# An encoder block on one core: its front stage in another order, its small preparations on other engines

## The chip, the cores and the metric

The kernel runs on one core of one Trainium2 chip. The metric is the device time of one execution in microseconds (us); the runs shown are three executions of the kernel before, and of them the median counts.

## What is computed

One layer of a bidirectional encoder for two sequences of 512 tokens and width 1024, all in fp32. Cut to what matters here:

```python
mod = silu(c) @ w_ada + b_ada            # conditioning: 6 x 1024 values per sequence
sh1, sc1, gt1, sh2, sc2, gt2 = split(mod, 6)
h = rmsnorm(x, g_attn) * (1 + sc1) + sh1
z = h @ w_in                             # -> qa, ka, va, cq, ckv, kr, gla, glb
qa, ka = rope(rmsnorm(qa, gq_a)), rope(rmsnorm(ka, gk_a))     # mixer A: 8 and 2 heads of 64
oa = window_attention(qa, ka, va, sink_a)
qb = rmsnorm(rmsnorm(cq, g_cq) @ w_uq, gq_b)                  # mixer B: low-rank parts, 256 wide
kv = rmsnorm(ckv, g_ckv) @ w_ukv                              # and 128 wide; 32 of a head's 96
ob = dense_attention(rope(qb), rope(norm(kv, kr, gk_b)), v)   # columns are rotated
mix = sigmoid(gla) * (oa @ w_o_a) + sigmoid(glb) * (ob @ w_o_b)
x = x + gt1 * (mix @ w_out)
# then a second modulated norm, and a gated MLP with a depthwise convolution of width 3
```

## The kernel before, in words

The engines are TensorE (PE), VectorE (DVE), ScalarE (ACT) and GpSimd (POOL); SP issues all DMAs, in order. Every fp32 operand of a large product is split into a rounded high part and the rest (hi, lo), and a product is three matmuls (mm3, L78 to L81): hi by hi, hi by lo, lo by hi. A framework takes the program's instructions, plans each engine's order by priority and a cost model of its own, gives out the buffers of a pool in turn (`bufs`), and adds the waits; each engine then runs its list strictly in order. Where a line stands in keep_in_program_order, the plan may not move it.

The front stage has these parts. Tokens lie in 8 tiles of 128 (NT = 4 for a sequence), the width in KD = 8 blocks of 128.

1. *Norm* (norm, L243): a tile of x is loaded; two ACT squares with sums, a mean, a reciprocal root by ACT's Sqrt and five DVE instructions (rsqrt, L83), and a DVE scaling (L254). The first sequence's four tiles come first, the second sequence's in steps 3 to 6 of the next part.
2. *Eight steps* (L269): step k loads 1 MB of w_ada0, makes the scale and shift of block k by 32 small matmuls (64 recorded, L281) and a transpose (L289), transposes block k of the first sequence (L104), modulates and splits it (modulated, L109), and multiplies block k - 1 by the weights of part 0 of w_in (project, L263: 12 matmuls of 416 columns into four PSUM banks). Part 0 holds cq, ckv and kr. POOL splits these weights. Behind step 7's load the rotary tables are loaded and multiplied by gains on DVE (tables, L190).
3. *Second sequence* (L301): eight blocks are transposed and modulated; in between the low-rank weights w_uq and w_ukv are loaded and split (low_rank, L218).
4. *Low-rank parts* (prep_b, L340), a generator in three stages, so that three tiles are under way: squares and roots of cq and ckv, cn = part of z by root by gain (L353) and the rotation of kr on POOL; transposes of cn (L360) and their split; products with w_uq and w_ukv, copies, squares, roots, rotation on POOL, scalings, and three DMAs to a DRAM scratch. Tiles 4 to 7 first need their own product z (z_tile, L329).
5. *Mixer A* (prep_a, L405): for part 1 and then part 2 of w_in, 384 columns each, and each tile: product z in one of two PSUM banks, ACT copy to SBUF, square, sum and root for 4 or 6 heads of 64, rotation in four DVE instructions (L324 to L327), scaling by the root (L426), DMAs to DRAM. In each of these 16 iterations stands one step of the second half of the conditioning (ada, L141): 1 MB of w_ada, four matmuls (8 recorded, L151); after eight of them an addition (L155), four transposes (L158) and copies.

Behind it the attention block begins: its tiles lie in the SBUF of parts 1 to 5. PE runs the attention of both mixers with the gate products (gates, L470, matmuls L491) spread between; POOL splits the gate weights (L69, L72). Two banks are theirs, six the attention's. Parts 1 to 3 hold all eight PSUM banks, part 5 three.

Of the kernel before, what the change touches and what calls it, by code (L numbers as in the profile page):

```python
# [8 lines left out]
F32 = mybir.dt.float32  # L9
# [30 lines left out]
def encoder_block(ctx, tc, x, c_t, w_ada0, b_col, w_ada, b_ada, cols, w_z, w_g, gains, tabs, sink,  # L40
# [18 lines left out]
    SY.dma_start(colt, cols)  # L59
# [5 lines left out]
    SY.dma_start(gcol[0:NOPE, 0:1], gains[2 * AD:2 * AD + NOPE].unsqueeze(1))  # L65
    SY.dma_start(gcol[0:NOPE, 1:2], gains[2 * AD + BQK:2 * AD + BQK + NOPE].unsqueeze(1))
# [16 lines left out]
    def rsqrt(pool, a, width):  # L83
# [43 lines left out]
    with ExitStack() as st:  # L127
# [9 lines left out]

        bcol = zp.tile([128, 2 * KD], F32, name="bcol")
        SY.dma_start(bcol, b_col)

        def ada():  # L141

            for part in range(2):
# [27 lines left out]
        def table(tc_, ts_, off, dim, g0):  # L171
# [5 lines left out]
            V.tensor_mul(tc_, tc_, bcast(g, 1, [128, NT, dim]))  # L177
            V.tensor_mul(ts_[:, :, 0:h], ts_[:, :, 0:h], bcast(g[:, h:dim], 1, [128, NT, h]))
            V.tensor_mul(ts_[:, :, h:dim], ts_[:, :, h:dim], bcast(g[:, 0:h], 1, [128, NT, h]))
# [8 lines left out]
        gbc = ur.tile([128, QL + KVL], F32, name="gbc")  # L188

        def tables():  # L190
            for m in range(2):
                table(tcb[:, :, m], tsb[:, :, m], 2 * AD, ROPE, 2 * AD + m * BQK + NOPE)
            SY.dma_start(gbc, gains[2 * AD + 2 * BQK:2 * AD + 2 * BQK + QL + KVL].partition_broadcast(128))

# [22 lines left out]

        def low_rank(k):  # L218

            rw = zp.tile([128, KD, 4, 64], F32, name="w_ada", bufs=3).rearrange("p a b c -> p (a b c)")  # L220
# [15 lines left out]
        with ExitStack() as s0:  # L236
# [6 lines left out]
            def norm(t):  # L243
                xt = wk.tile([128, D], F32, name="xt", bufs=2 * NT)
                SY.dma_start(xt, x[t * 128:(t + 1) * 128, :])
                ss = wk.tile([128, 2], F32, name="ss", bufs=4)
                for q in range(2):
                    junk = wk.tile([128, S], F32, name="tmp", bufs=2)
                    A.activation(junk, xt[:, q * S:(q + 1) * S], AF.Square, accum_out=ss[:, q:q + 1])
                r = wk.tile([128, 1], F32, name="r", bufs=4)  # L250
                V.tensor_add(r, ss[:, 0:1], ss[:, 1:2])
                mean_eps(r, r, D)
                rsqrt(wk, r, 1)
# [890 lines left out]
```

## Time and profile before

| | |
|---|---|
| runs shown | 1458.96, 1456.97, 1456.27 us; median 1456.97 |
| profiled execution | 1456.77 us, span 1455.0 us from first to last instruction |
| PE | 1391.8 us busy, 96% of the span |
| DVE, ACT, POOL | 1000.3, 679.3, 596.0 us busy |
| DMA | 193.82 MB, 133 GB/s on average |
| chain that ended last | PE 77%, DVE 13% |

The rows below are of five kinds. [...] A row of a wait names who waited for whom, the total, the number of times and the longest. A row in order of time has start, length, engine, line, operation, tiles, shapes, and in brackets the idle time before it and what ended it. A row of a group has the count behind x, the busy time, the mean of one in ns, and the idle time before them. A row of a DMA has the count, the size and the median time from issue to landing. PE's matmuls overlap, so that their lengths are longer than the distance from one to the next.

### The profile page before, as it was taken

How to read it: one execution, taken by the hardware profiler on the slowest of the kernel's cores; microseconds unless marked ns; L12 is line 12 of the kernel's file. 1: busy time of each engine (PE TensorE's matmuls, PEld its weight loads, DVE VectorE, ACT ScalarE, POOL GpSimd, SP SyncE). 2: the span in 40 equal slices, each digit the busy share in tenths (PEclk: the TensorE clock that was granted, in tenths of full speed). 3: DMA queues.
4: the chain of work that ended last, by engine and by line, in shares of the span. 5: the costliest groups of instructions: out<-in, count | busy, mean ns of one | idle time of the engine just before them, and what ended most of it. 6: DMA issues, size and time to landing. Idle time of an engine off the chain costs nothing.

```text
span 1455.0 us, 20795 instructions
## 1 busy us (share of the span) xinstructions
PE 1391.8 (96%) x7184; PEld 1153.1 (79%) x7184; DVE 1000.3 (69%) x1907; ACT 679.3 (47%) x1385; POOL 596.0 (41%) x592
## 2 busy tenths in 40 slices
PE   5888998999999999999998899999999999999998
PEld 4777776888888888878887767888888888888887
DVE  5788776666678886545479888777777787447433
ACT  3475223666666665422347455555555554212210
POOL 3174023442433442381005755555555545544430
PEclk9999999999999999999999999999999999999999
DMA  8565763322222213655312322222222327646522
GB/s 342 176 216 170 236 239 135 116 88 87 88 87 73 102 64 120 236 176 200 133 39 73 120 74 87 87 82 85 87 85 82 102 73 250 205 148 223 180 87 73
DMA packets 107801, 193.82 MB, mean 133 GB/s; under 512 B 18856, under 2 KB 39592, under 8 KB 104624
## 3 DMA queue, kind: packets, MB, share of 16 engines
q1 hardware_dynamic: 107696, 192.49, 39.8%
q8 instruction: 57, 0.93, 0.3%
q14 instruction: 48, 0.39, 0.1%
HBM read 148.39 MB, written 44.06 MB: 132 GB/s over the span
## 4 chain that ended last, share of the span: by engine, by line
PE 77%; DVE 13%; POOL 3%; ACT 2%; DMA 2%; issue 2%; SPq 0%; ACTq 0%; POOLq 0%; DVEq 0%
PE px L955 13%; PE psg L491 11%; PE py L955 7%; PE psd L79 5%; PE psd L80 5%; PE psd L81 5%; PE pz L955 3%; PE ppt L512 3%; PE ppo L575 2%; PE psx L81 2%; PE psx L80 2%; PE psx L79 2%; PE psz L79 2%; PE psy L81 1%; PE psy L79 1%
## 5 line engine op out<-in xcount | busy, mean ns | idle before, releaser
L955 PE MATMUL px<-t,wt 128*128 128x512 f32 x792 | 191.2, 391 | 7.0 <-ACT tmp_cc L960 6.3
L922 POOL TENSOR_TENSOR wt<-wraw,wt 128x512 fp32r<-128x512 f32 x66 | 92.8, 1410 | 232.2 <-ACT wt L921 232.0
L955 PEld LDWEIGHTS px<-t,wt 128*128 128x128 f32 x792 | 148.0, 188 | 41.1 <-ACT tmp_cc L960 9.5
L491 PE MATMUL psg<-h_hi,wg 128*128 128x512 f32 x512 | 170.2, 397 | 0.0
L506 POOL TENSOR_SCALAR p<-p,l 128x512 f32<-128x512 f32 (+2 forms) x128 | 78.8, 617 | 200.3 <-DVE l L505 125.7
L76 DVE TENSOR_TENSOR wd<-wraw,wd 128x512 fp32r<-128x512 f32 x88 | 93.1, 1098 | 96.4 <-ACT wd L75 96.4
L79 PE MATMUL psd<-wd 128*128 128x512 f32 x352 | 136.9, 389 | 0.0
L80 PE MATMUL psd<-wd 128*128 128x512 f32 x352 | 136.9, 389 | 0.0
L81 PE MATMUL psd<-wd 128*128 128x512 f32 x352 | 136.9, 389 | 0.0
L75 ACT CAST wd<-wraw 128x512 fp32r<-128x512 f32 x88 | 51.3, 620 | 156.1 <-issue 86.9
L491 PEld LDWEIGHTS psg<-h_hi,wg 128*128 128x128 f32 x512 | 95.9, 189 | 18.4 <-POOL wg L69 0.8
L491 PE MATMUL psg<-h_lo,wg 128*128 128x512 f32 x256 | 101.8, 397 | 0.0
L504 ACT ACTIVATE p<-pps,nm 128x512 f32<-128x512 f32 (+2 forms) x128 | 78.2, 611 | 39.3 <-DVE nm L501 31.7
L922 DVE TENSOR_TENSOR wt<-tmp_sf,wt 128x512 fp32r<-128x512 f32 x88 | 82.2, 944 | 12.2 <-ACT wt L921 12.0
L967 DVE SCALAR_TENSOR_TENSOR tmp_u<-tmp_cc,cw,tmp_u 128x511 f32<-128x511 f32 x66 | 64.3, 974 | 37.3 <-ACT tmp_u L966 37.2
L69 POOL TENSOR_SCALAR wd<-wraw 128x512 fp32r<-128x512 f32 x44 | 34.2, 777 | 112.0 <-PE psd L81 63.9
L81 PEld LDWEIGHTS psd<-wd 128*128 128x128 f32 x352 | 66.1, 188 | 13.8
L79 PEld LDWEIGHTS psd<-wd 128*128 128x128 f32 x352 | 66.1, 188 | 13.7
L80 PEld LDWEIGHTS psd<-wd 128*128 128x128 f32 x352 | 66.1, 188 | 13.6
L501 DVE TENSOR_REDUCE nm<-pps 128x1 f32<-128x512 f32 (+2 forms) x128 | 74.7, 584 | 3.1 <-PE pps L81 1.5
L966 ACT ACTIVATE tmp_u<-tmp_cc,cw 128x512 f32<-128x512 f32 x66 | 53.6, 813 | 45.7 <-DMA g_d<-tmp_u 25.6
L72 POOL TENSOR_TENSOR wd<-wraw,wd 128x512 fp32r<-128x512 f32 x44 | 72.7, 1653 | 3.7
(257 smaller groups left out, 3517.8 us busy)
## 6 DMA issues: line engine op xcount, KB each, us to landing
w_ada<-in_w_ada_dram SPq DMA_DIRECT2D x24, 1024.0 KB, 7.1
wraw<-in_w_up_dram SPq DMA_DIRECT2D x96, 256.0 KB, 2.7
wraw<-in_w_down_dram SPq DMA_DIRECT2D x88, 256.0 KB, 3.6
g_d<-tmp_u SPq DMA_DIRECT2D x44, 256.0 KB, 2.4
wraw<-g_d SPq DMA_DIRECT2D x44, 256.0 KB, 2.7
wg_raw<-in_w_g_dram SPq DMA_DIRECT2D x16, 512.0 KB, 3.7
gate_d<-go SPq DMA_DIRECT2D x32, 256.0 KB, 2.0
ldb<-qb_d SPq DMA_DIRECT2D x8, 1024.0 KB, 4.9
```

Source lines behind the costliest of these rows:

```text
L72: G.tensor_sub(lo, raw, hi.bitcast(F32))
L76: V.tensor_sub(lo, raw, hi.bitcast(F32))
L79: PE.matmul(ps, lhsT=lh, rhs=rh, start=first, stop=False)
L80: PE.matmul(ps, lhsT=lh, rhs=rl, start=False, stop=False)
L81: PE.matmul(ps, lhsT=ll, rhs=rh, start=False, stop=last)
L491: PE.matmul(ps, lhsT=w[:, wl, m, k, :], rhs=hl[b][:, k, :], start=k == 0 and n == 0, stop=k == KD - 1 and n == 2)
L501: V.tensor_reduce(nm, ps[:, :n], op=ALU.max, axis=AX.X, negate=True)
L504: A.activation(p[:, :n], ps[:, :n], AF.Exp, bias=nm, accum_out=l)
L506: G.tensor_scalar(out=p[:, :plen], in0=p[:, :plen], scalar1=l, scalar2=1.0, op0=ALU.mult, op1=ALU.mult)
L922: lo_eng.tensor_sub(w[:, 1], raw, w[:, 0].bitcast(F32))
L955: PE.matmul(ps[:, sl], lhsT=w[:, wl, i], rhs=h[:, hl, sl], start=not add and i == 0 and n == 0, stop=i == 3 and n == 2, skip_group_check=add)
L967: V.scalar_tensor_tensor(out=u[:, 1:S], in0=src[:, 0:S - 1], scalar=cw[:, cc, 0:1], in1=u[:, 1:S], op0=ALU.mult, op1=ALU.add)
```

## The change

The front stage is rebuilt. The x loads go ahead of the small ones; 60 transposes of the identity stand on PE's list ahead of the steps. Norms are made for two tiles at a time (first sequence) and four (second), with the scalings partly on ACT and the root by two instructions less. The squares' outputs go to tiles that are written later. The tables are multiplied on POOL, later. The gains of cq and ckv are folded into the low-rank weights' split, and cn becomes two ACT copies. The conditioning's second half runs between the low-rank parts, two steps per tile, its loads three ahead. The weights of parts 1 and 2 are loaded in two large pieces into the buffers of w_ada, and split later. Mixer A reads PSUM directly: four banks more, ACT scales each head by its root, DVE and POOL share the rotation, and the closing product is gone.

```diff
     def rsqrt(pool, a, width):
...
-        V.tensor_mul(u, a, y)
+        V.scalar_tensor_tensor(out=u, in0=a, scalar=-0.5, in1=y, op0=ALU.mult, op1=ALU.mult)
         V.tensor_mul(u, u, y)
-        V.tensor_scalar(out=u, in0=u, scalar1=-0.5, scalar2=1.5, op0=ALU.mult, op1=ALU.add)
-        V.tensor_mul(a, y, u)
+        V.scalar_tensor_tensor(out=a, in0=u, scalar=1.5, in1=y, op0=ALU.add, op1=ALU.mult)
...
         def ada():
+            ws = []
+            def load():
+                n = len(ws)
+                if n < 2 * KD:
+                    w = zp.tile([128, KD, 4, 64], F32, name="w_ada", bufs=3).rearrange("p a b c -> p (a b c)")
+                    SY.dma_start(w, w_ada[n // KD, n % KD])
+                    ws.append(w)
+            load()
+            load()
+            yield
             for part in range(2):
...
                 for k in range(KD):
-                    w = zp.tile([128, KD, 4, 64], F32, name="w_ada", bufs=3).rearrange("p a b c -> p (a b c)")
-                    SY.dma_start(w, w_ada[part, k])
+                    load()
+                    w = ws[part * KD + k]
...
-            V.tensor_mul(tc_, tc_, bcast(g, 1, [128, NT, dim]))
+            G.tensor_mul(tc_, tc_, bcast(g, 1, [128, NT, dim]))
...
+        def weights_late(part):
+            c0, cw = ZC[part]
+            raws = []
+            for k in range(0, KD, 4):
+                raw = zp.tile([128, KD, 4, 64], F32, name="w_ada", bufs=3).rearrange("p a b c -> p (a b c)")[:, :4 * cw]
+                raw = raw.rearrange("p (k n) -> p k n", k=4)
+                SY.dma_start(raw, w_z[:, k:k + 4, c0:c0 + cw])
+                raws.append(raw)
+            def split():
+                tiles = []
+                for k in range(KD):
+                    w, raw = zp.tile([128, 2, ZB], F32R, name="wz", bufs=10), raws[k // 4][:, k % 4]
+                    A.copy(w[:, 0, :cw], raw)
+                    (V if k % 2 else G).tensor_sub(w[:, 1, :cw], raw, w[:, 0, :cw].bitcast(F32))
+                    tiles.append(w)
+                return tiles
+            return split
...
-                tc.keep_in_program_order(A.copy(hi, raw))
-                tc.keep_in_program_order(V.tensor_sub(lo, raw, hi.bitcast(F32)))
+                tc.keep_in_program_order(A.activation(hi, raw, AF.Copy, scale=g))
+                tc.keep_in_program_order(V.scalar_tensor_tensor(out=lo, in0=raw, scalar=g, in1=hi.bitcast(F32),
+                                                                op0=ALU.mult, op1=ALU.subtract))
...
+            for t in range(NT):
+                load_x(t)
+            SY.dma_start(colt, cols)
+            SY.dma_start(bcol, b_col)
+            one = wk.tile([128, 1], F32, name="one")
+            V.memset(one, 1.0)
+            tc.keep_in_program_order(A.activation(one, one, AF.Sqrt))
+            for t in range(0, NT, 2):
+                ss = wk.tile([128, 2], F32, name="ss", bufs=2)
+                for j in range(2):
+                    xt = xn[t + j].rearrange("p (a n) -> p a n", a=2)
+                    A.activation(h_lo[1][:, 2 * (t + j):2 * (t + j) + 2, :], xt, AF.Square, accum_out=ss[:, j:j + 1])
+                r = scales(ss)
+                V.tensor_scalar(out=xn[t], in0=xn[t], scalar1=r[:, 0:1], scalar2=None, op0=ALU.mult)
+                if t:
+                    A.activation(xn[t + 1], xn[t + 1], AF.Copy, scale=r[:, 1:2])
+                else:
+                    V.tensor_scalar(out=xn[t + 1], in0=xn[t + 1], scalar1=r[:, 1:2], scalar2=None, op0=ALU.mult)
+            idle = pst.tile([128, S], F32, name="pst")
+            for j in range(60):
+                PE.transpose(idle[:, (j % NT) * 128:(j % NT + 1) * 128], ident, ident)
...
-                xt = transposed(pst, xn[:NT], k, True)
+                xt = transposed(pst, xf[:NT], k, True)
+                if k:
+                    project(k - 1, 0, 2)
...
                 if k:
-                    project(k - 1)
+                    project(k - 1, 2, NT)
...
+                if 2 <= k < 6:
+                    t = NT + k - 2
+                    A.activation(h_hi[1][:, 2 * (k - 2):2 * (k - 1), :], xn[t].rearrange("p (a n) -> p a n", a=2), AF.Square,
+                                 accum_out=ss1[:, k - 2:k - 1])
+                if k == 5:
+                    r1 = scales(ss1)
+                    for t in range(NT):
+                        A.activation(xn[NT + t], xn[NT + t], AF.Copy, scale=r1[:, t:t + 1])
...
-                    V.scalar_tensor_tensor(out=cn[:, c0:c1], in0=zt[:, c0:c1], scalar=rc[:, j:j + 1], in1=gbc[:, c0:c1],
-                                           op0=ALU.mult, op1=ALU.mult)
+                    A.activation(cn[:, c0:c1], zt[:, c0:c1], AF.Copy, scale=rc[:, j:j + 1])
...
+                for h in range(n):
+                    A.activation(zs[:, h], zh[:, h], AF.Copy, scale=rs[:, h:h + 1])
...
+                V.tensor_mul(t1, zv, tc_)
+                G.tensor_mul(t2[lo], zv[hi], ts_[lo])
+                G.tensor_mul(t2[hi], zv[lo], ts_[hi])
+                V.tensor_add(ov, t1, t2)
...
             for t in range(2 * NT + 2):
+                for _ in range(2):
+                    next(mods, None)
+                if t == 2 * NT - 1:
+                    later = weights_late(1)
                 if t < 2 * NT:
                     stages.append(prep_b(t, zfirst[t] if t < NT else z_tile(t, tiles, ZC[0][1])))
...
+                if t == 2 * NT:
+                    tiles = later()
...
+            pza = s0.enter_context(tc.tile_pool(name="pza", bufs=4, space=PSUM))
+            later = weights_late(2)
             for part in range(2):
-                tiles = weights(1 + part)
                 for t in range(2 * NT):
-                    prep_a(t, z_tile(t, tiles, ZC[1 + part][1]), part)
-                    next(mods, None)
-            for _ in mods:
-                pass
+                    zt = z_product(pza, t, tiles, ZC[1 + part][1])
+                    if not part and t == 2 * NT - 1:
+                        tiles = later()
+                    prep_a(t, zt, part)
```

## Rows read from the trace of the kernel before

**Rows 1.** Busy time of each engine by stretch, then clock, DMA share, GB/s.
```profile
14.50:61.10 46.60, 38.84 (x656) 33.16 (x657) 31.12 (x103) 14.47 (x34) 14.01 (x16) 0.96 0.71 255
...
61.10:75.10 14.00, 12.85 (x74) 10.71 (x71) 12.82 (x26) 10.25 (x24) 4.22 (x9) 1.00 0.82 288
...
75.10:140.50 65.40, 56.04 (x288) 47.56 (x288) 56.49 (x163) 43.49 (x117) 41.94 (x73) 0.97 0.54 179
...
140.50:216.30 75.80, 75.43 (x448) 59.55 (x446) 56.56 (x211) 19.82 (x53) 10.23 (x12) 1.00 0.75 244
...
216.30:225.50 9.20, 3.07 (x17) 2.35 (x14) 9.10 (x12) 0.34 (x2) 9.20 (x10) 0.78 0.49 170
...
225.50:400.00 174.50, 174.49 (x924) 145.41 (x923) 112.23 (x225) 107.38 (x227) 62.32 (x82) 0.99 0.29 100
...
10.00:40.00 30.00, 21.35 (x395) 18.30 (x395) 21.12 (x71) 11.83 (x32) 10.83 (x12) 1.00 1.02 401
```

**Rows 2.** Waits of PE, 75 to 232 us: us, times, longest.
```profile
PE ppr L360 <- DVE cn L353: 8.9, 6, 3.0
...
PE psa L158 <- DVE br L155: 6.1, 1, 6.1
```

**Rows 3.** PE in order of time, first steps: start, length, line, count.
```profile
14.52 1.94 PE L281 MATMUL pa<-w_ada,c_s 128*32 128x64 f32 x64 [14.52 <-DMA w_ada<-in_w_ada_dram]
...
21.90 1.11 PE L104 MATMUL pst<-ident,xt 128*128 128x128 f32 x4
...
25.77 1.10 PE L281 MATMUL pa<-w_ada,c_s 128*32 128x64 f32 x64
...
26.80 0.66 PE L104 MATMUL pst<-ident,xt 128*128 128x128 f32 x4
...
29.76 1.10 PE L281 MATMUL pa<-w_ada,c_s 128*32 128x64 f32 x64
```

**Rows 4.** As rows 1, stretches for the clock.
```profile
14.50:23.50 9.00, 6.72 (x139) 5.25 (x140) 6.76 (x19) 0.98 (x2) 5.16 (x7) 1.00 1.01 414
...
48.00:50.00 2.00, 2.00 (x49) 1.79 (x41) 0.41 (x2) 0.00 (x0) 0.00 (x0) 0.50 0.06 13
...
224.70:228.30 3.60, 3.54 (x11) 2.96 (x12) 3.57 (x14) 0.00 (x0) 2.18 (x2) 0.51 0.14 50
```

**Rows 5.** SP and PE in order of time, at the start.
```profile
3.55 1.85 SPq L245 DMA_DIRECT2D xt<-in_x_dram  x4
...
19.41 0.48 PE L104 MATMUL pst<-ident,xt 128*128 128x128 f32 x1 [2.12 <-DVE xt L254]
```

**Rows 6.** Groups of ACT, 75 to 140.5 us: count, busy us, mean ns.
```profile
L346 ACT ACTIVATE jc<-zo 128x128 f32<-128x128 f32 x7 | 2.1, 303 | 0.1
```

**Rows 7.** Groups of DVE, 75 to 140.5 us.
```profile
L353 DVE SCALAR_TENSOR_TENSOR cn<-zo,rc,gbc 128x256 f32<-128x256 f32 x8 | 5.7, 712 | 0.0
...
L353 DVE SCALAR_TENSOR_TENSOR cn<-zo,rc,gbc 128x128 f32<-128x128 f32 x8 | 3.6, 446 | 0.0
```

**Rows 8.** PE in order of time, conditioning beside mixer A.
```profile
199.10 1.07 PE L151 MATMUL psa<-w_ada,c_s 128*32 128x512 f32 x8
...
204.50 1.06 PE L151 MATMUL psa<-w_ada,c_s 128*32 128x512 f32 x8
```

**Rows 9.** DMA issues: count, KB each, median us to landing.
```profile
w_ada<-in_w_ada_dram SPq DMA_DIRECT2D x24, 1024.0 KB, 7.1
```

**Rows 10.** As rows 1, two tiles of mixer A.
```profile
199.70:205.10 5.40, 5.40 (x40) 4.32 (x32) 3.65 (x13) 1.21 (x3) 0.00 (x0) 1.00 0.87 293
...
210.50:219.90 9.40, 8.13 (x49) 5.93 (x41) 9.18 (x13) 1.73 (x4) 9.40 (x11) 1.00 0.23 75
```

**Rows 11.** Groups of DVE, 199.7 to 205.1 us.
```profile
L426 DVE TENSOR_TENSOR oa<-oa,rs 128x384 f32<-128x384 f32 x1 | 0.6, 558 | 0.0
```

**Rows 12.** Groups of POOL, 75 to 140.5 us.
```profile
L324 POOL TENSOR_TENSOR t1b<-qf,tcb 128x256 f32<-128x256 f32 x8 | 8.3, 1037 | 5.6 <-ACT qf L380 5.6
...
L325 POOL TENSOR_TENSOR t2b<-qf,tsb 128x128 f32<-128x128 f32 x8 | 4.4, 549 | 0.0
```

More of the change, by code (lines that the diff above doesn't have):

```diff
@@ L187, in encoder_block @@
         tsa = zp.tile([128, NT, 2, AD], F32, name="tsa")
-        gbc = ur.tile([128, QL + KVL], F32, name="gbc")
+        glr = zp.tile([128, 3], F32, name="glr")
         def tables():
@@ L241, in encoder_block, with load_x @@
             xn = [None] * (2 * NT)
-            def norm(t):
+            def load_x(t):
                 xt = wk.tile([128, D], F32, name="xt", bufs=2 * NT)
                 SY.dma_start(xt, x[t * 128:(t + 1) * 128, :])
[L246 to L253, printed above, removed]
-                V.tensor_scalar(out=xt, in0=xt, scalar1=r, scalar2=None, op0=ALU.mult)
-                xn[t] = lambda k, xt=xt: xt[:, k * 128:(k + 1) * 128]
@@ L257, in encoder_block, with scales, part_of @@
-            for t in range(NT):
-                norm(t)
+                xn[t] = xt
+            def scales(ss):
+                n = ss.shape[1]
+                r = wk.tile([128, 4], F32, name="r", bufs=3)[:, :n]
+                mean_eps(r, ss, D)
+                rsqrt(wk, r, n)
+                return r
+            def part_of(t):
+                return lambda k: xn[t][:, k * 128:(k + 1) * 128]
+            xf = [part_of(t) for t in range(2 * NT)]
+            for t in range(NT):
+                load_x(t)
@@ L267, in project, with second_batch @@
                         k == 0, k == KD - 1)
+            ss1 = wk.tile([128, NT], F32, name="ss1")
+            r1 = None
+            second = iter(range(KD))
+            def second_batch():
+                k = next(second, None)
+                if k is not None:
+                    modulated(wk, transposed(pst, xf[NT:], k), 1, a1, 0, h_hi[1], h_lo[1], k)
             for k in range(KD):
@@ L299, in encoder_block @@
                 modulated(wk, xt, 0, a1, 0, h_hi[0], h_lo[0], k)
-            project(KD - 1)
-            for k in range(KD):
-                split = low_rank(k // 2) if k % 2 == 0 else split
-                modulated(wk, transposed(pst, xn[NT:], k), 1, a1, 0, h_hi[1], h_lo[1], k)
-                if k % 2:
-                    split()
+                if 2 <= k < 6:
+                    t = NT + k - 2
[5 more added lines that the diff above has]
+                        A.activation(xn[NT + t], xn[NT + t], AF.Copy, scale=r1[:, t:t + 1])
+                if k == 7:
+                    second_batch()
+            project(KD - 1, 0, NT)
+            mods = ada()
+            splits = [low_rank(n) for n in range(2)]
+            tables()
+            for k in range(0, KD, 2):
+                if k == 4:
+                    splits += [low_rank(n) for n in range(2, 4)]
+                second_batch()
+                second_batch()
+                splits[k // 2]()
+            next(mods)
+            SY.dma_start(gcol[0:NOPE, 0:1], gains[2 * AD:2 * AD + NOPE].unsqueeze(1))
+            SY.dma_start(gcol[0:NOPE, 1:2], gains[2 * AD + BQK:2 * AD + BQK + NOPE].unsqueeze(1))
+            G.tensor_scalar(out=gcol[:, 1:2], in0=gcol[:, 1:2], scalar1=BQK ** 0.5, scalar2=1.0, op0=ALU.mult, op1=ALU.mult)
             zfirst = []
```

78 lines of the change are left out of this document (41 added, 37 removed).

## The prediction

> **What bounds the kernel now.** First the busy time by stretch [rows 1]. After 225.5 us TensorE (PE) is busy without a hole: 174.49 of 174.5 us up to 400. What fills it there are the gate products, which wait for nothing that the attention does; so a front stage that ends earlier should move everything behind it forward by the same amount, and the whole question is how early PE becomes dense. Before that, PE starts at 14.5 and is idle (length less busy time) for 7.8 us up to 61.1, 1.2 up to 75.1, 9.4 up to 140.5, 0.4 up to 216.3, and 6.1 of the 9.2 us up to 225.5: 24.8 us.
>
> Second the waits [rows 2]. The 9.4 us of the third stretch are almost all one wait: the transposes of the low-rank parts wait for the scaled rows cn, and VectorE (DVE) makes those late; it is busy 56.5 of 65.4 us there. The 6.1 us are another single wait: the last conditioning transposes (L158) stand in PE's queue and wait for one addition (L155) on DVE.
>
> Third the first steps of PE in order of time [rows 3], beside the granted clock [rows 4]. The 64 small conditioning matmuls of a step take 1.94 us in the first two steps (one is shown) and 1.10 from the third on; the four transposes of a step 1.11, then 0.66. In the first 9 us the clock row says 1.00, but these durations are those of the lower level, which the other rows show as 0.50; I go by the durations. The lower level costs 2 x (0.84 + 0.45) = 2.6 us in the first two steps, and about half of three later stretches of some 3.5 us each (two are shown, the third is at 116): 5.2. With the idle time PE loses 24.8 + 7.8 = 32.6 us in the front, and 14.5 before it begins. That is all there is to win.
>
> **The change part by part.** The profiled execution took 1456.77 us with a span of 1455.0; the median of the runs shown is 1456.97, 0.2 above it. The sum is made against 1456.77.
>
> *Start.* Four small DMAs go from in front of the x loads, which are issued at 3.55 us [rows 5]; four issues take 1.85 us there, so at most 1.9 us are won. Nothing is won if the 60 added transposes still hold PE when the first weights land. At the lower level one follows the other by about 0.21 us ((1.11 - 0.48) / 3, [rows 3, 5]), so 60 take 12.7 us from about 1.7: until 14.4, today's start. At the higher one they are done at about 10. The chain in front of the first transposes also shortens: today the fourth waits 2.1 us, until 19.41, for DVE's scaling of x [rows 5]; now sums and roots go two tiles at a time, the function table is loaded ahead, and one of the four scalings goes to ScalarE (ACT). I take 1.5 between the ends 0 and 1.9.
>
> *The eight steps of conditioning and projection.* They last 46.6 us from 14.5 to 61.1. A step with nothing in its way takes 29.76 - 25.77 = 4.0 us [rows 3]; eight make 32, the last chain from the transposes to the modulated block some 2.7 (0.66 and four instructions of about half a microsecond, an estimate), the last projection 2.3, what is left of a step without the small matmuls and transposes: 37. The norms of the second sequence, which ran one tile at a time through ACT and DVE between the steps, become one square per step, one root for four tiles and four ACT scalings; the tables leave this stage. Late next are the loads: 14.3 MB (4.2 of x, 8.4 of w_ada0, 1.7 of w_z) at 401 GB/s [rows 1] are 35.7 us, so the last weights land near 39, about when PE wants them (13 + 7 x 4.0 = 41). And the four 1024-wide scalings, each under 2.4 us by the 0.30 that ACT takes for 128 columns [rows 6], queue on ACT in front of step 6. I keep 2.5 us for both: 39.5, a gain of 7; ends 0 (loads and ACT late as before) and 9.6.
>
> *Second sequence.* Its scalings are in the stage above; transposes and splits stay, and the gains are folded into w_uq and w_ukv at the same number of instructions. Twelve table products leave DVE (12.8 of 14.0 us busy) and run on GpSimd (POOL), where they can slow DVE. I take 0; ends -3 (DVE slowed by a quarter) and +1.2 (all of the idle time).
>
> *Low-rank parts.* Per tile DVE loses the two cn products, 0.71 + 0.45 us [rows 7], and three or four tiny instructions of the roots and means; some 1.7 us, 14 over eight tiles: 56.5 falls to 42. ACT gets two copies for cn; 0.30 for the 128-wide one [rows 6], at most twice that for the 256-wide, so 0.9 x 8 = 7: 43.5 rises to 51. The sixteen conditioning steps move in, two per tile. A step costs PE 1.2 us: 1.07 and the gap ahead of it [rows 8]. A tile of mixer A with its step takes 5.40, without it 4.2, so 14 of the 16 tiles fit into today's 75.8 us behind 140.5; the other two and their 8 us, which fill holes here, go out, and 14 steps come in: PE has 56 + 17 - 8 = 65 us of work and more to do while cn is made. Sixteen loads of 1 MB come along, in three buffers, 7.1 us each to landing [rows 9]: three in flight make 2.4 us each, 38 for sixteen, so they fit; but each step stands in PE's queue and, if late, holds the low-rank products and the z tiles behind it, and SP's queue holds the loads among the writes of q, k and v. Of the 11.1 us lost here (9.4 idle, 1.7 of clock) I take 5 as won; ends -6 (eight steps late by 0.8 each) and 11.1.
>
> *Mixer A.* Its 16 tiles cost PE 4.2 us each instead of 5.4, which is only the 1.2 that moved. DVE's 3.65 us of busy time per tile [rows 10] lose the closing product, 0.56 [rows 11], and two half-wide ones, together the same: 2.5. POOL gets the two half-wide products, at 192 columns between 0.55 and 1.04 each [rows 12], 1.6 together. ACT gets six copies of 64 columns, each under 0.30, and has 1.21 today, 3.0 in all. Everything lies under 4.2, so PE stays the bound and the cost is 0. New is the border: the first weights of part 1 are loaded behind the last conditioning step, into its buffers, and their splits stand behind the low-rank work on ACT and DVE; PE has one tile's low-rank products to cover it. I charge 2; ends 0 and 5. The case that the three engines do not keep up is a rival below.
>
> *Tail.* With the conditioning early, L155 and L158 are out of the way: 6.1 idle and 1.8 of clock. Late next is the end of mixer A. Its four PSUM banks come on top of the three of this stage, so seven of eight are held until ACT has copied the last tiles out, and one of the two banks of the gate products may wait for that: square, reduction, root, five tiny DVE instructions, six copies, about 4 us behind the last product by the rows named. POOL must also split the first gate weights among its new products. I take 4 of 7.9 as won; ends 0 and 7.9.
>
> Sum: 1.5 + 7 + 0 + 5 - 2 + 4 = 15.5, so 1456.8 - 15.5 = 1441.3, say **1441**. All good ends together are 32 us (1425), all bad ones -14 (1471); as six parts rarely fall to one side, the likely case has 1433 to 1448.
>
> **The rivals.**
>
> *The transposes do not warm PE.* For it: the second step still runs at the lower level. Against: the higher one comes at about 23.5, when PE had done little but small matmuls and transposes since 20. If it holds, PE starts at 14.4 (1.4 lost) and the two slow steps stay (2.6), of which the loads hide part: 1444. [...]
>
> *The low-rank stage does not shorten.* ACT in order with 51 us, or sixteen loads that hold PE's queue, take the place of DVE. For it: DVE and ACT pass each tile back and forth, and the wait for cn would only change its name. Against: no engine but PE would be over 80% busy. Price: the 5 us and 2 more at the border, 1448; with the tail's stall kept too, 1452.
>
> *Slower: DVE stretched by POOL in mixer A.* Where POOL is busy all the time, from 210.5 to 219.9, DVE needs 9.2 us for the 13 instructions that it does in 3.65 beside an idle POOL [rows 10]: 2.5 times. If its 2.5 us stretched as much, a tile would take 6.3 instead of 4.2 and, with four banks full, hold PE: 16 x 2.1 = 33 us, so 1474. It decides where a tile passes 5.2 us, as 16 x 1.0 eats the gain. Against: POOL would be busy 1.6 of 4.2 us, in which DVE does 0.6 of its 2.5; 3.5 us is what the rows give. [...]
>
> *More than forecast.* Nearly all idle time goes: 1425 to 1433. For it: PE has filler everywhere; against: new dependences in every part.
>
> **How the numbers follow.** Forecast 0.50; cold transposes 0.13; low-rank stage unchanged 0.17; more 0.08; slower, by POOL or another stall of that size, 0.12. Within 0.2% (2.9 us, about what a measurement can tell from no change) lies a fifth of the low-rank case and a little of the last: same 0.05; slower 0.10; faster 0.85. The range leaves out the slow end and the best one: 1429 to 1455.
>
> **What would show it.** First small matmuls at 12 to 13 us and 1.1 us long (1.9: the cold rival). The eighth step's projection ends near 52, not 61. The wait for cn falls under 5 us. No wait of PE for L155. Mixer A's tiles follow each other by 4.2 to 4.4 us; 5 or more is the slow rival. PE is dense from about 210. The forecast is wrong if the front ends early but PE has holes behind it, or if PE waits for w_ada in the low-rank stage for more than a few us.

## The result: 0.9% slower, where 1.1% faster was forecast

The changed kernel takes 1472.28 us (median of 4 runs, 1469.09 to 1475.48), the kernel before 1457.24 beside it (4 runs); the ratio is 1.0094, interval 1.0076 to 1.0112. The forecast was 1441 in a range of 1429 to 1455. (The ratio is the one on record; the quotient of the medians, 1.0103, differs a little.) The profiled execution took 1471.41 us, 14.6 more than that of before.

The busy time by stretch of the changed kernel, columns as in [rows 1]: the two ends and the length, then for PE, PEld (weight loads), DVE, ACT and POOL the busy time and the instructions, then PE's granted clock as a share of full speed, the busy share of the DMA engines and GB/s:

```profile
139.50:197.80 58.30, 49.65 (x239) 46.82 (x240) 38.76 (x96) 17.27 (x69) 33.40 (x42) 0.85 0.46 138
197.80:223.40 25.60, 25.60 (x147) 25.32 (x145) 11.39 (x36) 9.50 (x39) 7.63 (x10) 1.00 0.11 32
223.40:240.00 16.60, 3.29 (x9) 2.58 (x9) 6.82 (x23) 5.39 (x23) 4.51 (x6) 0.57 0.13 39
240.00:400.00 160.00, 160.00 (x845) 133.50 (x844) 99.38 (x193) 97.50 (x206) 57.68 (x77) 0.99 0.28 95
```

PE is dense from 240.0; before it was from 225.5 [rows 1]. The 14.5 us between are the whole loss, and they arise behind 139.5, in mixer A. By then all sixteen conditioning steps are done, and none of the sixteen tiles; before, 14 tiles with a step each lay behind 140.5. The sixteen tiles are 16 x 4.2 = 67.2 us of PE's work, so PE could have been dense at 206.7, 18.8 earlier than before. It gets there 33.3 us later than that: 8.7 idle in the first row (length less busy time), 13.3 idle in the third, whose 3.3 busy are gate products already, and 49.65 + 25.60 - 67.2 = 8.0 more than 4.2 a tile. Most of that goes with the granted clock, which is 0.85 on average in the first row: 0.50 from 139 to 143 and from 183 to 195, each time behind a wait of PE, and 1.00 from 195 to 223. Matmuls of 384 columns follow each other by 0.32 us at 0.50 (from 188 on) and by 0.17 or 0.18 at 1.00 (from 196 on); half of the 13.2 us that PE is busy at 0.50 makes an estimate of 6.6 of the 8.0. The waits of PE up to 262 us (us, times, longest) name the places:

```profile
PE psg L592 <- ACT zs L503: 13.3, 1, 13.3
PE psz L76 <- DVE h_hi L109: 6.1, 4, 2.5
PE psz L76 <- ACT vf L465: 5.3, 1, 5.3
PE psz L76 <- ACT wz L236: 4.2, 2, 3.7
PE psz L76 <- ACT v L527: 3.0, 2, 1.9
...
PE psa L164 <- DVE br L161: 0.9, 1, 0.9
...
PE ppr L443 <- ACT cn L437: 0.9, 2, 0.5
```

The wait for vf, the copy that empties the bank of the last low-rank tile, ends at 139.51, ahead of the first row. The 8.7 idle in that row are the waits for wz, the split weights (the longest ends at 183.39, at the border between part 1 and part 2), and for v, the last copy out of a bank of mixer A. The last two lines are what the forecast wanted: the wait for cn falls from 8.9 to 0.9, that for L155 (now L161) from 6.1 to 0.9 [rows 2]. The first line is new: the first gate product needs a PSUM bank that ACT has not yet emptied, and ACT empties the last tiles late, because the tiles come late. ACT, DVE and POOL in part 2 of mixer A, each in order of time:

```profile
208.61 1.34 ACT L503 ACTIVATE zs<-psz,rs 128x64 f32<-128x64 f32 x6 [0.92 <-DVE rs L88]
209.80 0.52 ACT L492 ACTIVATE sq<-psz 128x384 f32<-128x384 f32 x1
212.84 0.21 ACT L84 ACTIVATE rsq_y<-rs 128x6 f32<-128x6 f32 x1 [2.52 <-DVE rs L499]
213.97 1.34 ACT L503 ACTIVATE zs<-psz,rs 128x64 f32<-128x64 f32 x6 [0.92 <-DVE rs L88]
```
```profile
210.02 0.97 POOL L517 TENSOR_TENSOR t<-zs,tsa 128x192 f32<-128x192 f32 x1 [3.84 <-ACT zs L503]
210.96 0.59 POOL L518 TENSOR_TENSOR t<-zs,tsa 128x192 f32<-128x192 f32 x1
```
```profile
209.98 0.56 DVE L516 TENSOR_TENSOR t<-zs,tca 128x384 f32<-128x384 f32 x1 [1.46 <-ACT zs L503]
211.58 0.56 DVE L519 TENSOR_TENSOR oa<-t,t 128x384 f32<-128x384 f32 x1 [1.04 <-POOL t L518]
212.05 0.55 DVE L494 TENSOR_REDUCE rs<-sq 128x6 f32<-128x384 f32 x1
212.63 0.17 DVE L499 TENSOR_SCALAR rs<-rs 128x6 f32<-128x6 f32 x1
213.08 0.19 DVE L85 RECIPROCAL rsq_y<-rsq_y 128x6 f32<-128x6 f32 x1 [0.28 <-ACT rsq_y L84]
...
213.71 0.17 DVE L88 SCALAR_TENSOR_TENSOR rs<-rsq_u,rsq_y 128x6 f32<-128x6 f32 x1
```

Read it as one ring. ACT scales a tile out of PSUM (zs, 1.34); POOL makes its two products (0.97 + 0.59); DVE adds (0.56) and only then reduces the squares of the *next* tile, which ACT wrote at 209.80 and which have lain there for 1.7 us; then the root on ACT (0.21), four small instructions on DVE, and ACT may scale that next tile, at 213.97. From 208.61 that is 5.36 us, and all tiles of part 2 follow each other by 5.33 to 5.46. No engine is busy half of it: DVE 11.39 of 25.6 us, ACT 9.50, POOL 7.63 in the second row above. Every duration is undisturbed; the engines take turns. PE, with 4.2 us of work per tile, runs ahead into the four banks: its last product is done at 223.4, the last tile leaves its bank only from 235.36 on, and until then PE stands.

Part 1 has a shorter ring (four heads) and still takes 6.3 to 6.5 us a tile (zs at 164.40, 170.94, 177.26; the next, with POOL free of splits, comes 4.31 later). There POOL also splits gate weights, which the planner has put between its products. First the groups of DVE from 156 to 181 us, then one of these kinds in part 2 (count, busy us, mean ns), then POOL in order of time:

```profile
L519 DVE TENSOR_TENSOR oa<-t,t 128x256 f32<-128x256 f32 x5 | 4.0, 807 | 3.8 <-POOL t L518 3.8
L87 DVE TENSOR_TENSOR rsq_u<-rsq_u,rsq_y 128x4 f32<-128x4 f32 x3 | 3.6, 1213 | 0.1
L86 DVE SCALAR_TENSOR_TENSOR rsq_u<-rs,rsq_y 128x4 f32<-128x4 f32 x4 | 2.8, 702 | 0.1
...
L85 DVE RECIPROCAL rsq_y<-rsq_y 128x4 f32<-128x4 f32 x4 | 0.7, 178 | 1.1 <-ACT rsq_y L84 1.1
```
```profile
L87 DVE TENSOR_TENSOR rsq_u<-rsq_u,rsq_y 128x6 f32<-128x6 f32 x7 | 1.2, 166 | 0.2
```
```profile
166.74 1.36 POOL L66 TENSOR_SCALAR wg<-wg_raw 128x512 fp32r<-128x512 f32 x2
168.08 2.55 POOL L69 TENSOR_TENSOR wg<-wg_raw,wg 128x512 fp32r<-128x512 f32 x2
171.95 0.70 POOL L517 TENSOR_TENSOR t<-zs,tsa 128x128 f32<-128x128 f32 x1 [1.32 <-ACT zs L503]
```

L87 works on 4 elements per partition (6 in part 2), and takes 1.21 us beside the splits and 0.17 without them; 1.21 is about the length of one L69 on POOL (2.55 for two). The reciprocal, with one input, stays at 0.18 beside the same L69 (at 168.50 and 174.83); not every instruction with one input does (last section).

### The profile page after: what moved, and what is told of

The parts are those of the page before. It is cut to its first block, busy times and chain, and to the rows that moved or that the text cites. A ratio compares the mean times of both kernels' runs of the same rounds, so it can differ in the third digit from the quotient of the medians.

```text
span 1469.6 us, 20912 instructions
## 1 busy us (share of the span) xinstructions
PE 1403.4 (95%) x7244; PEld 1165.1 (79%) x7244; DVE 971.3 (66%) x1734; ACT 697.8 (47%) x1458; POOL 611.8 (42%) x633
## 4 chain that ended last, share of the span: by engine, by line
PE 73%; DVE 10%; issue 4%; POOL 4%; ACT 2%; DMA 2%; ACTq 0%; POOLq 0%; DVEq 0%; SPq 0%
PE px L1056 13%; PE psg L592 11%; PE py L1056 6%; PE psd L78 5%; PE psd L76 5%; PE psd L77 5%; PE pz L1056 3%; PE ppt L613 3%; PE ppo L676 2%; PE psx L76 2%; PE psx L77 2%; PE psx L78 2%; PE psy L78 2%; PE psy L76 1%; PE psy L77 1%
## 5 line engine op out<-in xcount | busy, mean ns | idle before, releaser
L592 PE MATMUL psg<-h_hi,wg 128*128 128x512 f32 x512 | 171.0, 400 | 13.3 <-ACT zs L503 13.3
L1023 DVE TENSOR_TENSOR wt<-tmp_sf,wt 128x512 fp32r<-128x512 f32 x88 | 85.2, 977 | 11.8 <-ACT wt L1022 11.4
L1068 DVE SCALAR_TENSOR_TENSOR tmp_u<-tmp_cc,cw,tmp_u 128x511 f32<-128x511 f32 x66 | 63.7, 965 | 35.4 <-ACT tmp_u L1067 35.4
L76 PE MATMUL psz<-wz,h_hi 128*128 128x384 f32 (+1 forms) x176 | 64.8, 369 | 19.0 <-DVE h_hi L109 6.1
L1070 DVE SCALAR_TENSOR_TENSOR tmp_u<-tmp_cc,cw,tmp_u 128x511 f32<-128x511 f32 x66 | 74.2, 1124 | 1.4
```

The source lines that it names most:

```text
L76: PE.matmul(ps, lhsT=lh, rhs=rh, start=first, stop=False)
L592: PE.matmul(ps, lhsT=w[:, wl, m, k, :], rhs=hl[b][:, k, :], start=k == 0 and n == 0, stop=k == KD - 1 and n == 2)
L1023: lo_eng.tensor_sub(w[:, 1], raw, w[:, 0].bitcast(F32))
L1068: V.scalar_tensor_tensor(out=u[:, 1:S], in0=src[:, 0:S - 1], scalar=cw[:, cc, 0:1], in1=u[:, 1:S], op0=ALU.mult, op1=ALU.add)
L1070: V.scalar_tensor_tensor(out=u[:, 0:S - 1], in0=src[:, 1:S], scalar=cw[:, cc, 2:3], in1=u[:, 0:S - 1], op0=ALU.mult, op1=ALU.add)
```

## Experiments

Two theories stood at the start. *Ring*: mixer A's pace is a ring through three engines' queues, closed by the order of the instructions. *Contention*: DVE is slow because POOL works beside it. A third, that the chain starts late (its first square waits 5.1 us, until 152.35, for a buffer that a write still reads), came beside them. The table gives each kernel's median and its ratio to the kernel before, with its interval; the medians of before were 1457.4 to 1458.5 in the four sets. The ratios are those on record; quotients of the medians differ from them by up to 0.002 (0.9908 for e10).

| kernel | us | ratio |
|---|---|---|
| changed kernel | 1472.3 | 1.0094 [1.0076, 1.0112] |
| e1 old mixer A in the new front | 1450.1 | 0.995 [0.993, 0.997] |
| e2 lines moved | 1471.3 | 1.0091 [1.0075, 1.0108] |
| e3 new mixer A in the old front | 1474.2 | 1.0108 [1.0087, 1.0130] |
| e4 all products on DVE | 1464.6 | 1.0048 [1.0031, 1.0066] |
| e5 no transposes | 1471.6 | 1.0085 [1.0062, 1.0109] |
| e6 order forced | 1457.4 | 0.9989 [0.9975, 1.0003] |
| e7 e6, gate splits moved | 1449.2 | 0.9946 [0.9928, 0.9963] |
| e8 gate splits moved alone | 1468.9 | 1.0070 [1.0048, 1.0093] |
| e9 e7, first tiles' banks | 1450.0 | 0.9929 [0.9901, 0.9956] |
| e10 e9, gate products' banks | 1444.0 | 0.9887 [0.9858, 0.9915] |
| e12 e1, gate splits moved | 1447.9 | 0.9917 [0.9884, 0.9950] |
| e13 e7's mixer A in the old front | 1456.9 | 0.9991 [0.9972, 1.0010] |
| e14 gate products' banks alone | 1471.4 | 1.0093 [1.0069, 1.0117] |

**Is it mixer A?** e1 undoes it, e3 does it alone.

```diff
-                    zt = z_product(pza, t, tiles, ZC[1 + part][1])
+                    zt = z_tile(t, tiles, ZC[1 + part][1])
...
-            def prep_a(t, ps, part):
+            def prep_a(t, zt, part):
```

> The changed kernel with the mixer A of the kernel before (z copied out of two PSUM banks, the whole rotation on DVE in SBUF, nothing on POOL but the gate splits); the rest of the front stage as changed. Loop theory: in the changed kernel mixer A runs in a loop zs on ACT, t2 on POOL, add and the next tile's reduction on DVE, root on ACT, of 5.35 us a tile, against 4.2 us of PE work, and the last tile's banks hold the first gate product 13.3 us. Without it tiles follow each other by 4.2 to 4.6 us, the first gate product waits under 4 us, PE is dense from about 218 instead of 240, and the time is 1445 to 1452. Contention rival (DVE and POOL together are what is slow, the gate splits above all): the splits still run beside a DVE that has more to do, so tiles stay above 5 us and the time is 1460 or more. Late-start rival (the first square waits 5.1 us for a buffer that a write still reads, and the delay is never made up): that wait stays, so the gain is under 8 us, time 1464 to 1470.

1450.1: inside the ring theory's range, 22 us under the changed kernel. The squares in part 2, ACT in order of time, come every 4.21 us, PE's own pace:

```profile
203.81 0.53 ACT L492 ACTIVATE sq<-zo 128x384 f32<-128x384 f32 x1
...
208.02 0.53 ACT L492 ACTIVATE sq<-zo 128x384 f32<-128x384 f32 x1
```

The late start stays in it (the first square at 154.25), so that theory falls as the main cause.

> The kernel before with the new mixer A alone: products left in four PSUM banks, squares, copies and roots from there, two half-wide products on POOL; one conditioning step stays with each tile, and the front stage is as before. Loop theory: PE's work with its conditioning step is 5.4 us a tile, as long as the loop of 5.35, which is hidden there; only the end is left, where the first gate product waits some 5 us or more for a bank, of which the wait for L155 (6.1) already held a part. Time 1457 to 1464. Contention rival: DVE, stretched by POOL and by the conditioning additions of its own, passes 5.4 us in most tiles; time 1470 or more. Third: if the new mixer A by itself is good and only the front of the change hurts, 1455 or less.

1474.2: 16 us slower than before with nothing changed but mixer A. The range of the ring theory (1457 to 1464) is missed, and that of contention is hit. Part 2 does pass 5.4 only a little (zs every 5.57); it is part 1 that is lost, with the gate splits in it (ACT, first scaling of each tile):

```profile
174.19 0.93 ACT L431 ACTIVATE zs<-psz,rs 128x64 f32<-128x64 f32 x4 [3.65 <-DVE rs L92]
...
181.40 0.93 ACT L431 ACTIVATE zs<-psz,rs 128x64 f32<-128x64 f32 x4 [3.38 <-DVE rs L92]
...
188.96 0.93 ACT L431 ACTIVATE zs<-psz,rs 128x64 f32<-128x64 f32 x4 [1.26 <-DVE rs L92]
```

Over 7 us a tile, and PE then waits 9.9 us in all for the weights of part 2, whose splits stand on ACT and POOL behind the late tiles. So neither theory alone will do.

**The ring.** e2 issues the statistics of tile n+1 ahead of the rotation of tile n, by moving lines only:

```diff
-                    prep_a(t, zt, part)
+                    it = prep_a(t, zt, part)
+                    next(it)
+                    next(last, None)
+                    last = it
```

> The changed kernel with one thing moved: in mixer A the square, reduction, root and reciprocal of tile t+1 are issued ahead of the copies and rotation of tile t, on every engine's queue. Work, engines, buffers and banks are the same. Loop theory: the order is what closes the loop (the next reduction stands behind this tile's add in DVE's order), so tiles of part 2 follow each other by 4.2 to 4.5 us instead of 5.35, part 1 by under 6, the wait of the first gate product falls from 13.3 to 3 to 7, and the time from 1472 to 1450 to 1460. Contention rival: the same instructions run beside each other, so tiles stay at 5.0 or more and the time within 4 us of 1472. Late-start rival: part 1 starts as late, part 2 follows PE; gain under 5 us.

Nothing moves, but it decides nothing: the framework plans each engine's order itself and put the reduction of a tile behind the addition of the one before, as in the changed kernel; part 2 still goes by 5.36. e4 shortens the ring by taking POOL out of it:

```diff
-                G.tensor_mul(t2[lo], zv[hi], ts_[lo])
-                G.tensor_mul(t2[hi], zv[lo], ts_[hi])
+                V.tensor_mul(t2[lo], zv[hi], ts_[lo])
+                V.tensor_mul(t2[hi], zv[lo], ts_[hi])
```

> The changed kernel with the two half-wide products of mixer A on DVE instead of POOL; the order is kept. Loop theory: the products on POOL (0.97 + 0.60 us beside DVE's 0.56) become two of about 0.3 on DVE behind the full-wide one, so the loop gets 0.3 to 0.5 us shorter, about 4.9 a tile in part 2, and the gain is 16 x 0.4 = 6, time 1463 to 1469, with PE's waits still there. Contention rival: POOL is then free of all but the gate splits, DVE is not slowed, tiles fall to 4.2 to 4.5 and the time under 1458.

1464.6, the ring theory's range. DVE does more, and the tiles still come faster:

```profile
202.20 1.34 ACT L503 ACTIVATE zs<-psz,rs 128x64 f32<-128x64 f32 x6 [0.86 <-DVE rs L88]
...
206.78 1.34 ACT L503 ACTIVATE zs<-psz,rs 128x64 f32<-128x64 f32 x6 [0.86 <-DVE rs L88]
```

4.58 us: the ring lost 0.78, more than the 0.3 to 0.5 expected, and is still above 4.2. e6 forces the order that e2 meant, and puts the addition another tile later:

```diff
+            pin = tc.keep_in_program_order
...
-                A.activation(sqv, zh, AF.Square)
+                pin(A.activation(sqv, zh, AF.Square))
...
+                yield
                 zs = wk.tile([128, 6, AD], F32, name="zs", bufs=3)
...
+                yield
+                pin(V.tensor_add(ov, t1, t2))
...
-                    prep_a(t, zt, part)
+                    flight.insert(0, prep_a(t, zt, part))
+                    for it in flight:
+                        next(it, None)
+                    flight = flight[:2]
```

> The changed kernel with mixer A's order forced on ScalarE, VectorE and GpSimd, which moving the lines alone did not do (the planner put them back): statistics of tile n, copies and products of tile n-1, addition of tile n-2, in this order on each queue. Same work, engines and banks. Loop theory: no instruction of a tile waits any more for the same tile's step on another engine, so part 2 follows PE at 4.2 to 4.4 us a tile instead of 5.35, the first gate product waits under 5 us instead of 13.3, and the time is 1450 to 1458 (part 1 keeps its splits of gate weights). Contention rival: the same instructions stand beside the same GpSimd work; part 1 stays near 6.3 a tile, part 2 over 4.8, the time over 1464.

1457.4, in the ring theory's range, 15 us less with the same work on the same engines. Part 2 goes by 4.21 (ACT, first scaling of each tile), and the first gate product waits 4.1 instead of 13.3:

```profile
202.60 1.32 ACT L506 ACTIVATE zs<-psz,rs 128x64 f32<-128x64 f32 x6
...
206.82 1.32 ACT L506 ACTIVATE zs<-psz,rs 128x64 f32<-128x64 f32 x6
```

This is the run that shows the ring (the copy v also gets a third buffer in it, and which part of the new order does most was not taken apart). Part 1 stays uneven, between 3.7 and 6.5 us a tile in its middle.

**The splits.** e7 adds to e6, and e8 to the changed kernel, that the first gate weights are split between POOL's products of tiles 2 to 5 of part 2, the second ones behind mixer A:

```diff
+                    if part and t >= 2:
+                        next(wg0, None)
...
-                        split_pool(w[:, 0, m, k:k + 4], w[:, 1, m, k:k + 4], raw[:, k:k + 4])
+                        split_pool(w[:, 0, m, k:k + 4], w[:, 1, m, k:k + 4], raw[:, k:k + 4], f == 1)
```

> The forced order, and the splits of the first gate weights moved on GpSimd out of part 1 of mixer A, one quarter each behind the products of tiles 2 to 5 of part 2; those of the second gate weights behind mixer A. Loop theory alone: the order already lets the tiles follow PE, so this is within 3 us of the forced order alone. Both causes at work (loop in part 2, splits in part 1): part 1 falls from about 6 to 4.2 to 4.6 us a tile, another 6 to 10 us are won, time 1442 to 1449.

> The changed kernel, its order kept, with the gate splits alone moved as in the one before. Contention theory: part 1 falls from 6.3 to 4.6 us a tile or less and part 2 to under 5, 1450 to 1458. Loop theory: part 1 falls to about 4.5 (its loop is shorter, with four heads for six), part 2 stays at 5.35 or goes above it where a quarter of a split stands ahead of a product on GpSimd; what part 1 gains is given back, 1464 to 1473.

e7 takes 1449.2, 0.0043 (6 us) under e6, at the upper end of what was expected of both causes together. In both parts the tiles follow at 4.16 away from the border, and in part 2 ACT waits for PE's product before it squares:

```profile
167.66 0.91 ACT L506 ACTIVATE zs<-psz,rs 128x64 f32<-128x64 f32 x4
...
171.82 0.91 ACT L506 ACTIVATE zs<-psz,rs 128x64 f32<-128x64 f32 x4
...
199.69 0.49 ACT L494 ACTIVATE sq<-psz 128x384 f32<-128x384 f32 x1 [1.41 <-PE psz L78]
```

e8 takes 1468.9, as the ring theory had it: part 1 falls from 6.3 to 4.31 (its ring undisturbed: L87 takes 0.16 or 0.17 from 163 to 177), and part 2 gives it back where a quarter of a split stands in POOL's queue, 6.3 a tile. The end waits longer than in the changed kernel:

```profile
168.38 0.93 ACT L503 ACTIVATE zs<-psz,rs 128x64 f32<-128x64 f32 x4 [0.90 <-DVE rs L88]
...
172.69 0.93 ACT L503 ACTIVATE zs<-psz,rs 128x64 f32<-128x64 f32 x4 [0.89 <-DVE rs L88]
...
210.36 1.33 ACT L503 ACTIVATE zs<-psz,rs 128x64 f32<-128x64 f32 x6 [0.92 <-DVE rs L88]
...
216.63 1.34 ACT L503 ACTIVATE zs<-psz,rs 128x64 f32<-128x64 f32 x6 [0.92 <-DVE rs L88]
```
```profile
PE psg L612 <- ACT zs L503: 18.9, 1, 18.9
```

So contention was real, 2 us a tile in part 1. While the ring stood, moving the splits won some 3 us (the intervals of e8 and the changed kernel overlap); with the ring open it is worth 6. e12 moves the splits beside the old mixer A.

> The changed front with the mixer A of the kernel before (1450.1) and the gate splits moved out of part 1. If the splits on GpSimd slow VectorE, the old mixer A, which has all its rotation there, gains too: part 1 from about 5 to 4.3 us a tile, 1443 to 1447. If they only kept the new mixer A's own products waiting on GpSimd's queue, it stays at 1449 to 1451.

Its part 1 goes by 4.24 us, but PE waits 4.9 us for wz, 3.1 ahead of part 1 and 1.8 at the border to part 2; 1447.9 lies between the two ranges, 2 under e1 (5 by the ratios), and the intervals overlap, so the time decides nothing. It lies beside e7, so the new mixer A, mended, is not shown to beat the old one at all.

**The end.** e14 moves one line in the changed kernel, so that the gates' banks are not those of mixer A:

```diff
+        psg = st.enter_context(tc.tile_pool(name="psg", bufs=2, space=PSUM))
         pps = st.enter_context(tc.tile_pool(name="pps", bufs=2, space=PSUM))
...
-        psg = st.enter_context(tc.tile_pool(name="psg", bufs=2, space=PSUM))
```

> The changed kernel with one line moved: the gate products' two PSUM banks are taken first in their stage, so that they lie on banks that mixer A does not use. Its loop of 5.35 us a tile stays. If the lost time is PE's wait for the last tiles' banks (13.3 us, and the lower clock behind it, some 3 us more), the gates fill it, PE is dense from 223 instead of 240, and the time falls by 10 to 15, to 1457 to 1462. If what counts is when mixer A's results are there for the attention, which the loop sets, the gates done early leave PE a hole later: under 4 won, 1468 to 1472.

1471.4: the second. The gates start at 223.3, fill their two banks, and stop at 234.4. PE's waits from 195 us on:

```profile
PE ppt L652 <- DMA gate_d<-go: 6.8, 1, 6.8
PE psg L592 <- ACT go L596: 4.5, 1, 4.5
```

Their copies stand on ACT's list behind the last scalings (237.0), and the first load for the attention on SP's behind the last write of mixer A:

```profile
240.90 0.42 SPq L524 DMA_DIRECT2D qa_d<-oa  x1
...
243.37 0.43 SPq L639 DMA_DIRECT2D ldb<-qb_d  x1
```

So the wait of 13.3 us was a symptom: filled, it came back as two others (6.8 and 4.5). Banks matter once the ring is open:

> The forced order with the gate splits moved (1449.2), and the first two products of mixer A put into the two PSUM banks that the z tiles had, which are free by then, in place of two of its own four. There PE waited 5.4 us for the copy of the last tile's v out of the banks that mixer A takes over. If that wait is what is lost there, two tiles (8.4 us of work) cover it and 4 to 5.4 us are won: 1444 to 1446. If the first square, which comes at 152 for another reason (its buffer lies on one that a DMA still reads), sets the pace, the wait moves to the fifth or sixth product and nothing is won: 1448 to 1450.

> The same, and the two banks of the gate products taken first when that stage opens its pools, so that they lie on the banks of the z tiles and not on those of mixer A's last tiles. If the wait of 4.2 us of the first gate product and the lower clock behind it (0.83 from 210 to 220) are lost time, another 4 to 5 us are won: 1439 to 1442. If PE finds another wait in their place (the weights of the gates, whose last split stands behind the products of tile 13, or the scores), less than 1.5.

```diff
-                    zt = z_product(pza, t, tiles, ZC[1 + part][1])
+                    zt = z_product(psz if part == 0 and t < 2 else pza, t, tiles, ZC[1 + part][1])
```

e9, with this edit, shows no gain: its wait of 5.4 us goes, and one for the splits of mixer A's first weights (wz on DVE, 3.1) takes its place, not one at the fifth or sixth product. e10, with e14's line too, takes 1444.0, 6 under e9 and 2 above its range, which had counted on a gain of e9; PE is at work without a hole from 210 to 220, at a granted clock of 1.00 where e7 had 7.92 us busy at 0.83:

```profile
210.00:220.00 10.00, 10.00 (x46) 8.27 (x45) 4.42 (x10) 3.58 (x15) 5.14 (x9) 1.00 0.35 108
```

It beats both kernels: 0.9887 of the one before.

**The rest of the change.** e13 puts e7's mixer A under the old front, with a conditioning step at each tile.

> The front stage of the kernel before (the sixteen conditioning steps of the second half stand between mixer A's tiles) with the new mixer A in the forced order and the gate splits moved (roots in four instructions instead of five everywhere). It gives the worth of the rest of the change, against 1449.2 with both. Loop theory: with its order mended the new mixer A costs nothing beside 5.4 us of PE work a tile, against 16 us as it stands in the change; time 1453 to 1459, and the new front is worth 4 to 10. If the conditioning steps in between still bring the chain to a stop (the additions on VectorE stand in its order), 1464 or more.

1456.9, the ring theory's range: mended, the new mixer A costs nothing there. Against e7, which was timed in another set, the new front is worth 0.0045, 6.6 us.

**The transposes.** e5 leaves them out.

```diff
-            for j in range(60):
-                PE.transpose(idle[:, (j % NT) * 128:(j % NT + 1) * 128], ident, ident)
```

> The changed kernel without the 60 transposes on PE ahead of the first conditioning step. If they raise PE's clock for the first steps (the first small matmuls took 1.10 us behind them, 1.94 before), the first two steps take 0.8 and 0.4 us longer each without them, 2.6 us in all, and the time goes up by 1 to 3. If the loads set the pace of the steps, or mixer A sets the end whatever comes before it, nothing moves (within 1 us). If the transposes only hold PE, it goes down by up to 2.

1471.6, no change that the intervals could show, although the first small matmuls are shorter behind them. With them, in the changed kernel, and without (PE in order of time):

```profile
8.81 2.35 PE L306 MATMUL pst<-ident 128*128 128x128 f32 x20
11.33 1.10 PE L340 MATMUL pa<-w_ada,c_s 128*32 128x64 f32 x64 [0.18 <-ACT rsq_y L84]
```
```profile
12.06 1.93 PE L337 MATMUL pa<-w_ada,c_s 128*32 128x64 f32 x64 [12.06 <-DMA w_ada<-in_w_ada_dram]
```

1.10 against 1.93 us. What becomes of it later is not shown: the gain that was expected, 1 to 3 us, is inside the spread of the times (1468 to 1475 for the two kernels) and of the traces (the first scaling of mixer A starts at 155.67 here, at 154.59 in the changed kernel, and at 156.28 in e14, which has the same front).

## Why the prediction was wrong

*The step that failed* is the one on mixer A: "Everything lies under 4.2, so PE stays the bound and the cost is 0." Each engine's busy time was about right: 2.5 us of DVE forecast, and 2.5 is the sum of the rows above for an undisturbed tile; POOL 1.6 and 1.56, ACT 3.0 and 2.1. But busy time per engine bounds a loop only if the engines may run ahead of each other. The new mixer A hands each tile from ACT to POOL and DVE and back, and the planned order let the chain of one tile hardly overlap the next; the sum along the ring, 5.36, is the pace. The old mixer A had its rotation on one engine, and 5.4 us of PE work to hide behind. The prediction's own sign of being wrong, an early front with holes in PE behind it, is what came. The case lost 1.0094 - 0.9946 = 0.0148, 21.6 us, by it: 15 by the order (e6), 6 by the splits (e7).

*The slower rival* named the place, the bound (5.2 us) and, for part 1, the number, 6.3 us a tile by DVE stretched beside POOL. That the number was met is luck: the rival had DVE full, and DVE is busy 13.4 of the 20 us from 160 to 180; what takes 6.3 is the ring, lengthened by the stretched instructions in it. The rival was put aside because POOL's own products fill only 1.6 of 4.2 us. The trace of before showed POOL busy with the gate splits at the end of mixer A [rows 10], and the working for the tail names them among the new products; that they could move forward into part 1, once SP and the buffers are free, was not asked. From 160 to 180 us POOL was busy 16.7 of 20. Beside the splits L86, L87 and L519 take up to 1.27, 1.22 and 1.50 us (at 161.27, 162.58 and 158.69); in e8, with the splits moved away, 0.16, 0.16 and 0.42 (at 172.04, 172.24 and 170.54). The trace of before could already show that instructions of the root, on 6 elements, are stretched by 1 us, and that a reduction is not. DVE beside the gate splits there, in order of time:

```profile
211.79 0.54 DVE L413 TENSOR_REDUCE rs<-sq 128x6 f32<-128x384 f32 x1
...
213.17 1.25 DVE L95 TENSOR_SCALAR rs<-rs 128x6 f32<-128x6 f32 x1
...
217.26 1.20 DVE L92 TENSOR_TENSOR rs<-rsq_y,rsq_u 128x6 f32<-128x6 f32 x1
```

Beside an idle POOL, in the first stretch of [rows 10], these three take 0.54, 0.16 and 0.17.

*The border* (2 charged, 0 to 5): ahead of mixer A PE waits 5.3 for vf, which the prediction did not see. The wait for wz that was charged hides behind it: e9, without the first, shows 3.1. The 3.7 for wz in the table of waits stand at the border between part 1 and part 2, for which nothing was charged. *The tail* (4 won) is wrong by sign: with the ring PE waits 13.3 there; with the order forced 4.1, as its working had it.

*The front.* The start won 3.2 us, not 1.5 (first small matmuls at 11.33, before at 14.52 [rows 3]); the rival of cold transposes, with 1.9 us for these matmuls, is refuted by their 1.10. With the start, the eighth step comes only 5.2 us earlier (49.54 against 54.70), where 8.5 were forecast, so the steps gave 2.0 of their 7: PE waits four times for the modulated block h_hi, 6.1 us in all (2.4 before). From its first matmul to the end of the second sequence PE is idle 8.9 us, as before; only its busy time fell, by 2.0 (from 51.69 to 49.66), near the prediction's estimate for the longer matmuls and transposes of the first two steps (2.6). The second sequence ends 5.2 earlier too (69.9 against 75.1 [rows 1]), a gain of 0 as forecast; in the low-rank stage the waits went as forecast, and no load held PE for more than 1.1 us. At the end of the kernel the front is worth 6.6 us (e13 against e7, some 4 either way by their intervals), about half of the 13.5 that its terms add up to (7.7 by the medians). e10 is 16.5 us under the kernel before, near the 15.5 forecast (13.4 by the medians), but 6 of these come from banks that the change did not move.

## What to carry to other kernels

Where a tile's work is passed between engines, add up the handover path of one tile beside the busy time of each engine: if the next tile can't start before this one has gone round, the sum is the pace, however idle the engines. Moving an operation to an idle engine lengthens that path, and takes another place in a queue where later work may be planned in front of it. Filler that the tensor engine had between tiles hides such a ring; before moving it away, ask what the ring's pace is without it.

## What the runs showed of the hardware

In the changed kernel the DVE instruction L87, with two inputs of 4 elements per partition, takes 1.21 us on average from 156 to 181 us, beside POOL's L69, also with two inputs, of 1.29; it takes 0.16 at 181.12, beside an idle POOL, and 0.16 or 0.17 in e8, with the splits moved away. Of the instructions with one input some lengthen too: in the kernel before, beside the same splits, a TENSOR_SCALAR on 6 elements (L95) took 1.25 in place of 0.16, while a reduction kept its 0.54. What sets these kinds apart, no run shows.

The 60 transposes of the identity come at 6 or 7 a us between 3 and 7 us of the trace, with nothing else on PE, and at 11 a us from 8 on; the 64 small matmuls behind them take 1.10 us. In e5, where PE had done nothing before, these take 1.93. In the kernel before they take 1.94 in the first step [rows 3], and 1.90 from 47.24 on, where the granted clock falls to 0.50 (48 to 50 [rows 4]). In the first stretches that clock is shown as 1.00, in the changed kernel as in the one before [rows 4], and so says nothing here: that the transposes raise PE's clock is an estimate from the durations.
